# Tying the issue of a half-tile load to a point of the arithmetic, near the end of the store ahead of it

## The chip, the cores and the metric

One core of one Trainium2 chip runs the program. The metric is the device time of an execution in microseconds. The kernel before takes 161.46 us (161.22 to 161.59, three runs).

## The reference

```python
# x: (16, 512, 16, 64) fp32; cos, sin: (512, 32) fp32
x1, x2 = x[..., :32], x[..., 32:]
first  = x1[..., :16] * cos[..., :16] - x1[..., 16:] * sin[..., :16]
second = x1[..., :16] * sin[..., :16] + x1[..., 16:] * cos[..., :16]
out = concatenate([first, second, x2], axis=-1)
```

Half of every row is rotated and the other half is copied. The input is 33.55 MB and so is the output: all of it must be read from HBM (the chip's main memory) into SBUF (the core's working memory) and written back.

## The kernel before

The data is cut into four tiles of 8.39 MB (128 partitions, 16 rows of 1024 numbers each). A ring of three tiles lies in SBUF; VectorE, the engine that does the arithmetic, works in place, in pieces of eight rows (tile 2's second half in five and three). SyncE issues the loads and most of the stores; the DMA engines move the data. Tile 3 takes the place of tile 0 and so has to wait until tile 0 is stored. Tile 2 has a place of its own from the start, but its second half is loaded only behind the first store, so that the DMA engines have work while SyncE waits for that store to land.

```python
def load(t, lo=0, hi=K):
    return nc.sync.dma_start(out=rows(t, lo, hi), in_=xf[t, :, lo * R : hi * R])

def store(t, lo=0, hi=K, queue=nc.sync):
    return queue.dma_start(out=of[t, :, lo * R : hi * R], in_=rows(t, lo, hi))
# ... (tables of cos and sin are loaded and spread)
load(0); load(1); load(2, 0, KC)          # KC = 8, K = 16, KM = 13
# ...
rotate(0, 0, KC)      # four VectorE instructions: mul (L96), mul (L97), sub (L98), add (L101)
rotate(0, KC, K)
store(0)
load(2, KC, K)
load(3)
rotate(1, 0, KC)
rotate(1, KC, K)
behind_loads = store(1)
rotate(2, 0, KC)
near = rotate(2, KC, KM)
rotate(2, KM, K)
store(2, queue=nc.gpsimd)
# behind_loads is made to wait for near ("the store follows the loads at the DMA engines")
rotate(3, 0, KC)
rotate(3, KC, K)
store(3)
```

So the kernel already holds one transfer back: the store of tile 1 waits for a point in tile 2's arithmetic close to the end of the last load.

Of the kernel before, what the change touches and what calls it, by code (L numbers as in the profile page):

```python
# [1 line left out]

# [4 lines left out]


@with_exitstack
def kernel(  # L10
    ctx: ExitStack,
    tc: tile.TileContext,
    x: bass.AP,
    cos: bass.AP,
    sin: bass.AP,
    out: bass.AP,
):
    nc = tc.nc
    fp32 = mybir.dt.float32
    P = 128  # L20
    B, S, H, D = x.shape
    Q = D // 4
    HF = D // 2



    K = 16
    T = B * S // (P * K)
    PB = S // K
    REP = P // PB  # L30
    R = H * D
    NS = 3
    KC = K // 2
    KM = 13

    xf = x.rearrange("b s h d -> (b s h d)").rearrange("(t p f) -> t p f", t=T, p=P)
    of = out.rearrange("b s h d -> (b s h d)").rearrange("(t p f) -> t p f", t=T, p=P)
    cosf = cos.rearrange("(p k) j -> p (k j)", k=K)
    sinf = sin.rearrange("(p k) j -> p (k j)", k=K)

    const_pool = ctx.enter_context(tc.tile_pool(name="const", bufs=1))
    b_pool = ctx.enter_context(tc.tile_pool(name="bp", bufs=1, space=bass.MemoryType.PSUM))


    ring = const_pool.tile([P, NS, K, H, D], fp32)
    stage = const_pool.tile([P, 2, K, HF], fp32)
    spun = const_pool.tile([P, 2 * K, Q], fp32)
    packed = const_pool.tile([PB, 2 * K, Q], fp32)
    table = const_pool.tile([P, 2, K, 2, Q], fp32)

    def rows(t, lo, hi):
        return ring[:, t % NS, lo:hi].rearrange("p k h d -> p (k h d)")
# [8 lines that stand above are left out]
    nc.vector.memset(stage[:, :, :, 0:Q], 0.0)  # L61
    spread = stage.rearrange("(j b) t k i -> j b t (k i)", b=REP)
    nc.gpsimd.dma_start(out=spread[:, 0, 0], in_=cosf)  # L63
    nc.gpsimd.dma_start(out=spread[:, 0, 1], in_=sinf)  # L64
    load(0)
    load(1)
    load(2, 0, KC)




    PQ = PB // REP
    nc.vector.stream_shuffle(  # L73
        out=spun[:],
        in_=stage.rearrange("p t k j -> p (t k) j")[:, :, 0:Q],
        mask=[j % PQ * REP for j in range(PB)],
    )
    for q in reversed(range(REP)):
        n = PQ * (q + 1)
        nc.vector.tensor_copy(out=packed[0:n], in_=spun[q * PB : q * PB + n])  # L80

    for r in range(REP):
        nc.vector.tensor_copy(  # L83
            out=table[r * PB : (r + 1) * PB].rearrange("p t k c j -> p (t k) c j"),
            in_=packed.unsqueeze(2).to_broadcast((PB, 2 * K, 2, Q)),
        )
    C = table[:, 0].rearrange("p k c j -> p k (c j)")
    Sn = table[:, 1].rearrange("p k c j -> p k (c j)")

    def rotate(t, lo, hi):  # L90
        x1 = ring[:, t % NS, lo:hi, :, 0:HF]
        c = C[:, lo:hi].unsqueeze(2).to_broadcast((P, hi - lo, H, HF))
        s = Sn[:, lo:hi].unsqueeze(2).to_broadcast((P, hi - lo, H, HF))
        b_full = b_pool.tile([P, KC, H, HF], fp32, name="b_t")
        b_t = b_full[:, 0 : hi - lo]
        nc.vector.tensor_mul(out=b_t, in0=x1, in1=s)  # L96
        nc.vector.tensor_mul(out=x1, in0=x1, in1=c)  # L97
        nc.vector.tensor_sub(  # L98
            out=x1[:, :, :, 0:Q], in0=x1[:, :, :, 0:Q], in1=b_t[:, :, :, Q:HF]
        )  # L100
        return nc.vector.tensor_add(  # L101
            out=x1[:, :, :, Q:HF], in0=x1[:, :, :, Q:HF], in1=b_t[:, :, :, 0:Q]
        )

    rotate(0, 0, KC)
    rotate(0, KC, K)
    store(0)
    load(2, KC, K)
    load(3)
    rotate(1, 0, KC)  # L110
    rotate(1, KC, K)
    behind_loads = store(1)
    rotate(2, 0, KC)
    near = rotate(2, KC, KM)
    rotate(2, KM, K)
    store(2, queue=nc.gpsimd)

    tc.add_manual_dep(
        behind_loads.ins,
        near.ins.name,  # L120
        mybir.DependencyInfo(mybir.DependencyClass.Sync, mybir.DependencyReason.DATA),
        reason="the store follows the loads at the DMA engines",
    )
    rotate(3, 0, KC)
    rotate(3, KC, K)
    store(3)


# [1 line left out]
_INS = ['x', 'cos', 'sin']  # L130
_OUTS = [((16, 512, 16, 64), 'float32')]


# [23 lines left out]
```

## Time and profile before

| | before |
|---|---|
| median time | 161.46 us |
| span of the profiled run | 159.5 us |
| VectorE busy | 112.9 us, 71% |
| DMA engines busy, both queues | 98.1% |
| bytes read and written | 33.69 and 33.55 MB |

The prediction below shows the lines of this profile. One more view is used throughout, the trace's packet records: each of the 16 engines moves a tile as packets of one partition row, 64 KB for a whole tile (2.418 us each when nothing disturbs) or 32 KB for a half tile (1.213 us). What a packet takes beyond that, averaged over the 16 engines, is time lost on the DMA path (the **excess**). These records are in the packed trace; `prof` sums them up but doesn't print them one by one.

I call the place where a transfer of one direction follows one of the other a **seam**.

### The profile page before, as it was taken

To read this page: it belongs to the slowest core of one execution; us is meant where nothing else is said; L and a number is where in the kernel's file an instruction comes from. 1 tells how busy PE (TensorE), PEld (TensorE's weight loads), DVE (VectorE), ACT (ScalarE), POOL (GpSimd) and SP (SyncE) were. 2 spreads that over 40 slices of the span, in tenths; PEclk is the share of its full clock that TensorE was granted. 3 is DMA by queue.
4 is the path that set the end of the run, shared out by engine and by line. 5 is a ranking of instruction groups with operands and counts; after the bars stand their busy time and mean duration, and the time that the engine had idled before them with its cause. 6 is when DMAs were issued, how large, how long until landed. Compare 5 with 4: busy or idle time off the path is not lost.

```text
span 159.5 us, 115 instructions
## 1 busy us (share of the span) xinstructions
DVE 112.9 (71%) x47; POOL 1.9 (1%) x7
## 2 busy tenths in 40 slices
DVE  1000959999999999999999999999999990000000
POOL 3000000000000000000000000010000000000000
DMA  7969979899699699699996996996996996998966
GB/s 263 542 263 542 444 345 526 362 427 526 271 493 551 263 526 526 263 395 427 493 526 263 526 526 263 526 526 263 526 526 263 526 510 279 526 427 362 526 263 263
DMA packets 1360, 67.24 MB, mean 422 GB/s; under 512 B 176, under 2 KB 176, under 8 KB 208
## 3 DMA queue, kind: packets, MB, share of 16 engines
q1 hardware_dynamic: 1152, 58.72, 85.7%
q0 software_dynamic: 208, 8.52, 12.4%
HBM read 33.69 MB, written 33.55 MB: 422 GB/s over the span
## 4 chain that ended last, share of the span: by engine, by line
DVE 61%; DMA 14%; issue 5%; DVEq 1%
DVE b_t L96 22%; DVE ring L97 22%; DMA ring<-in_x_dram 14%; DVE ring L101 10%; DVE ring L98 7%; DVEq L152 1%; DVEq L96 0%
## 5 line engine op out<-in xcount | busy, mean ns | idle before, releaser
L96 DVE TENSOR_TENSOR b_t<-ring,table 128x4096 f32<-128x4096 f32 (+2 forms) x9 | 35.6, 3959 | 2.1 <-DMA ring<-in_x_dram 1.9
L97 DVE TENSOR_TENSOR ring<-ring,table 128x4096 f32<-128x4096 f32 (+2 forms) x9 | 35.6, 3950 | 0.3
L98 DVE TENSOR_TENSOR ring<-ring,b_t 128x2048 f32<-128x2048 f32 (+2 forms) x9 | 18.4, 2050 | 0.3
L101 DVE TENSOR_TENSOR ring<-ring,b_t 128x2048 f32<-128x2048 f32 (+2 forms) x9 | 18.4, 2043 | 0.0
L73 DVE LOAD_MASK_SELECT spun<-stage x1 | 0.0, 14 | 14.4 <-DMA stage<-in_sin_dram 14.4
L83 DVE COPY table<-packed 32x1024 f32<-32x1024 f32 x4 | 2.7, 684 | 0.1
L58 POOL DMA_DIRECT2D out_dram<-ring x1 | 0.6, 559 | 101.7 <-DVE ring L101 101.7
L80 DVE COPY packed<-spun 32x512 f32<-32x512 f32 (+3 forms) x4 | 1.7, 416 | 0.1
L61 DVE MEMSET stage<- 128x512 f32 x1 | 0.5, 485 | 0.9 <-PEq L141 0.9
L73 DVE STREAM_SHUFFLE spun<-stage 128x512 f32<-128x512 f32 x1 | 0.7, 722 | 0.0
L63 POOL DMA_DIRECT2D stage<-in_cos_dram x1 | 0.6, 642 | 1.3 <-DVE stage L61 1.3
L64 POOL DMA_DIRECT2D stage<-in_sin_dram x1 | 0.5, 532 | 0.0
L141 POOL MEMSET const-bfloat16-1.0<- 128x1 bf16 x1 | 0.1, 101 | 0.0
L141 POOL MEMSET const-float32-0.0<- 128x1 f32 x1 | 0.1, 98 | 0.2 <-issue 0.2
L141 POOL MEMSET const-float32-1.0<- 128x1 f32 x1 | 0.1, 98 | 0.0
L141 POOL MEMSET const-uint8-127<- 128x1 uint8 x1 | 0.1, 98 | 0.0
## 6 DMA issues: line engine op xcount, KB each, us to landing
ring<-in_x_dram SPq DMA_DIRECT2D x2, 4096.0 KB, 40.7
stage<-in_cos_dram POOLq DMA_DIRECT2D x1, 64.0 KB, 8.9
stage<-in_sin_dram POOLq DMA_DIRECT2D x1, 64.0 KB, 13.3
ring<-in_x_dram SPq DMA_DIRECT2D x3, 28.9
out_dram<-ring SPq DMA_DIRECT2D x3, 27.4
out_dram<-ring POOLq DMA_DIRECT2D x1, 39.5
```

Source lines behind the costliest of these rows:

```text
L58: return queue.dma_start(out=of[t, :, lo * R : hi * R], in_=rows(t, lo, hi))
L61: nc.vector.memset(stage[:, :, :, 0:Q], 0.0)
L63: nc.gpsimd.dma_start(out=spread[:, 0, 0], in_=cosf)
L64: nc.gpsimd.dma_start(out=spread[:, 0, 1], in_=sinf)
L73: nc.vector.stream_shuffle(out=spun[:], in_=stage.rearrange("p t k j -> p (t k) j")[:, :, 0:Q], mask=[j % PQ * REP for j in range(PB)],)
L80: nc.vector.tensor_copy(out=packed[0:n], in_=spun[q * PB : q * PB + n])
L83: nc.vector.tensor_copy(out=table[r * PB : (r + 1) * PB].rearrange("p t k c j -> p (t k) c j"), in_=packed.unsqueeze(2).to_broadcast((PB, ...
L96: nc.vector.tensor_mul(out=b_t, in0=x1, in1=s)
L97: nc.vector.tensor_mul(out=x1, in0=x1, in1=c)
L98: nc.vector.tensor_sub(out=x1[:, :, :, 0:Q], in0=x1[:, :, :, 0:Q], in1=b_t[:, :, :, Q:HF])
L101: return nc.vector.tensor_add(out=x1[:, :, :, Q:HF], in0=x1[:, :, :, Q:HF], in1=b_t[:, :, :, 0:Q])
L152: with _tile.TileContext(nc) as tc:
```

## The change

The load of tile 2's second half (the **half load**) is no longer queued right behind the first store, with all of that store's 20 us still ahead. It is issued when the first multiply of tile 1's second half ends, about three microseconds ahead of the end of the store. The same helper replaces the tie of the second store, which keeps its point.

```diff
-        nc.vector.tensor_mul(out=b_t, in0=x1, in1=s)
+        begun = nc.vector.tensor_mul(out=b_t, in0=x1, in1=s)
...
-        return nc.vector.tensor_add(
+        done = nc.vector.tensor_add(
...
+        return begun, done
+    def behind(transfer, point):
+        tc.add_manual_dep(transfer.ins, point.ins.name, ...)
...
     store(0)
-    load(2, KC, K)
+    rest = load(2, KC, K)
     load(3)
     rotate(1, 0, KC)
-    rotate(1, KC, K)
-    behind_loads = store(1)
+    behind(rest, rotate(1, KC, K)[0])
+    last = store(1)
     rotate(2, 0, KC)
-    near = rotate(2, KC, KM)
+    behind(last, rotate(2, KC, KM)[1])
...      (the old tc.add_manual_dep of the second store is removed)
```

More of the change, by code (lines that the diff above doesn't have):

```diff
@@ L100, in rotate @@
         )
-        return nc.vector.tensor_add(
+        done = nc.vector.tensor_add(
             out=x1[:, :, :, Q:HF], in0=x1[:, :, :, Q:HF], in1=b_t[:, :, :, 0:Q]
+        )
+        return begun, done
+    def behind(transfer, point):
+        tc.add_manual_dep(
+            transfer.ins,
+            point.ins.name,
+            mybir.DependencyInfo(
+                mybir.DependencyClass.Sync, mybir.DependencyReason.DATA
+            ),
+            reason="issue the transfer near the end of the one in front of it",
         )
@@ L107 @@
     store(0)
-    load(2, KC, K)
+    rest = load(2, KC, K)
     load(3)
     rotate(1, 0, KC)
-    rotate(1, KC, K)
-    behind_loads = store(1)
+    behind(rest, rotate(1, KC, K)[0])
+    last = store(1)
     rotate(2, 0, KC)
-    near = rotate(2, KC, KM)
+    behind(last, rotate(2, KC, KM)[1])
     rotate(2, KM, K)
     store(2, queue=nc.gpsimd)
-    tc.add_manual_dep(
-        behind_loads.ins,
-        near.ins.name,
-        mybir.DependencyInfo(mybir.DependencyClass.Sync, mybir.DependencyReason.DATA),
-        reason="the store follows the loads at the DMA engines",
-    )
     rotate(3, 0, KC)
```

## The prediction

> **What bounds the kernel now.** One core, 161.46 us (161.22 to 161.59). I read the head of the page first, then the DMA queues, then bandwidth by stretch, and only then the chain.
>
> ```profile
> span 159.5 us, 115 instructions
> DVE 112.9 (71%) x47; POOL 1.9 (1%) x7
> q1 hardware_dynamic: 1152, 58.72, 85.7%
> q0 software_dynamic: 208, 8.52, 12.4%
> HBM read 33.69 MB, written 33.55 MB: 422 GB/s over the span
> ```
>
> VectorE is busy for 71% of the span. The two DMA queues hold the 16 DMA engines for 85.7 + 12.4 = 98.1% of it. The bytes are the problem's own: four tiles of 8.39 MB read once and written once, 67.1 MB. The only open question is whether the rate could be higher. I cut the span at the packets' own starts (a window that cuts packets gives false swings, which is why the 40 slices of the page read 263 and 526 in turn). Columns: length, VectorE and GpSimd busy, a clock of no use here, DMA share, GB/s.
>
> ```profile
> 26.80:38.90 12.10, 12.00 (x5) 0.00 (x0) 1.00 1.00 433
> 53.40:65.50 12.10, 12.00 (x5) 0.00 (x0) 1.00 1.00 433
> 65.50:73.25 7.75, 7.68 (x3) 0.00 (x0) 1.00 0.99 406
> 73.25:80.50 7.25, 7.21 (x3) 0.00 (x0) 1.00 1.00 434
> 107.05:128.80 21.75, 21.58 (x7) 0.00 (x0) 1.00 1.00 434
> 133.70:155.50 21.80, 0.00 (x0) 0.00 (x0) 1.00 1.00 433
> ```
>
> Loads alone (first row), the first store alone (second), two stores from two queues (fifth): all run at 433 to 434 GB/s with the engines full. VectorE is idle in the last row and the rate is the same, so VectorE does not share in the bound. One row is lower: 406 GB/s between 65.50 and 73.25, where the first store ends and tile 2's second half (I call it **the half load**) begins. That is the place the change touches.
>
> ```profile
> 49.87 0.35 SPq L58 DMA_DIRECT2D out_dram<-ring  x1
> 49.88 4.43 DVE L96 TENSOR_TENSOR b_t<-ring,table 128x4096 f32<-128x4096 f32 x1
> 50.26 21.82 SPq L55 DMA_DIRECT2D ring<-in_x_dram  x2
> 63.33 4.43 DVE L96 TENSOR_TENSOR b_t<-ring,table 128x4096 f32<-128x4096 f32 x1
> SPq L55 <- DMA out_dram<-ring: 21.0, 1, 21.0
> ```
>
> The first four lines are the timeline, the last is SyncE's own waits. SyncE issues the first store at 49.87 and the half load at 50.26; the merged "x2" ends with the load of tile 3, which waited 21.0 us for the store to land and was issued at 71.76. The chain of waits on the page is 61% VectorE and only 14% DMA; I discount it, because it follows the last instruction back through VectorE and does not account for the last store's 27 us of data. The last store is issued at 131.19 and lands at 158.58, since the two stores ahead of it are still moving.
>
> **What the Trainium skill says.** "DMA: Bandwidth & Descriptors", section "Where 436 GB/s comes from", gives a ceiling of 435.2 GB/s for a core's 16 DMA engines; the 433 to 434 above agrees, so no reordering can raise the rate of the full stretches. The same page, "Queues, rings and completion order", says descriptors of one queue are consumed in ring order on each engine. The trace agrees: the half load was issued 0.4 us behind the store, yet the store landed 21.9 us after its issue (71.7) and the half load 31.1 us after (81.3), 9.6 us later, its own 4.19 MB at full rate. "Perfetto Trace Analysis", section "DMA Instruction — HWDGE (DVE, Sync)", says the profiled window of a DMA excludes the data movement; the trace agrees, 0.35 us of issue against 21.9 us to landing. No page says what a read queued behind a write on the same queue costs at the seam.
>
> **The change part by part.**
>
> *Removed:* nothing. Same instructions, same bytes, same queues. The tie of the second store to tile 2's 5-row piece is only rewritten through the helper.
>
> *Added:* one wait, of SyncE, on the first multiply of tile 1's second half. That multiply already posts its completion to VectorE's counter in the trace, so VectorE pays nothing. On the path: 0 us.
>
> *Moved:* the half load's issue, from 50.26 to the end of that multiply, 63.33 + 4.43 = 67.76, plus some 0.03 us: 67.79. VectorE runs without a gap from 22.99, so this moment does not move by itself.
>
> *Is the issue in time?* In the trace's packet records the store's last 64 KB packets start between 67.93 and 68.45 and end between 70.74 and 71.25 (landing 71.74). On an idle queue at the start of the kernel, the first load was issued at 0.74 and its first packets began at 1.74 to 2.17: 1.0 to 1.4 us. So the half load can begin at 67.79 + 1.0 to 1.4 = 68.8 to 69.2, which leaves 1.5 us before the earliest engine is free. No bubble.
>
> *What follows it on SyncE:* the tile 3 load still waits for the store's landing at 71.74, 3.5 us after the half load's issue is over (67.79 + 0.43 = 68.22). Its data is not due until the half load is through at 80.5, so there are about 9 us to spare. The half load itself is due when VectorE writes the second half of tile 2 at 90.2, against landing at 81.3: 9 us of slack. Tile 3 lands at 100.7 and is used at 104.3. All stay as they are.
>
> *What can be gained:* only the seam. The 65.50 to 73.25 stretch moved 406 x 7.75 = 3147 KB, which at 433 GB/s would take 7.27 us: 0.48 us lost, read at the first engine. Averaged over the engines, the packet records say less: the sixteen last store packets took 2.42 to 3.32 us in place of 2.418, 0.31 us in the mean, and the first load packets another 0.04: 0.35 us. The seams the other way, load to store at 51 and at 100, show packets at 2.42 us, no loss. So the intent must be that a load queued early takes something from the store in front at its end. If all of it came back: 161.46 - 0.35 = 161.1.
>
> The sum of the parts: 0 on the path, between 0 and -0.35 at the seam.
>
> **The rivals.**
>
> *A, the seam is inherent.* A read following writes costs 0.3 us however long it has been queued: by the time the last packets run (from 68.8) the half load is queued in either version. For: the loss falls on the last packets alone, and the store's earlier packets, with the load queued behind them for 18 us, took exactly 2.418. Against: the last packets that started earliest (67.93 to 68.28) suffered most, and these begin before the delayed load could arrive, so they might be spared. Time 161.4 to 161.5.
>
> *B, the early queueing caused it,* and the delay gives it back: 161.1. For: the point just made. Against: nothing in the trace shows how an engine would see so far ahead.
>
> *C, a cold start takes its place.* The kernel's first packets took 2.89 to 3.45 us, median 3.16, 0.74 more than later ones. If the load is queued too late to be read ahead, a cost of this kind could replace the 0.35: 161.8. Against: 1.5 us of lead, more than the issue needs. If the store, now alone, ended 1 us earlier, the lead would shrink but hold.
>
> *D, a late VectorE delays the load.* A chain of VectorE work now sets when data starts moving. Each us that multiply ends beyond about 70 costs a us of idle DMA. Against: its input landed at 42.2 and it starts at 63.33 behind unbroken work; nothing slower is in sight.
>
> **Range and chances.** I weigh A at 0.55, B at 0.3, C and D together at 0.15. With 161.45, 161.1 and 161.8 that gives 88.80 + 48.33 + 24.27 = 161.40. Three runs of the kernel before spread over 0.37 us, as much as the whole effect, so 8 in 10 lie between 160.9 and 161.8. Faster by 2% would need 3.2 us; the DMA engines' idle time in all the span is about 159.5 x 1.9% = 3.0 us, most of it ahead of the first packet and behind the last, so no version with these bytes can do it. Slower by 2% would need rival D at 3 us. Chances: faster 0.01, same 0.98, slower 0.01.
>
> **What would show it.** Right: SyncE's half load at about 67.8, the tile 3 load at about 71.7, the last store still at 131.2 and landing near 158.5, VectorE's busy time 112.9, and windows over the middle again at 433. The seam tells A from B: about 406 GB/s in the 7.75 us behind 65.5 is A, 420 or more is B, under 395 is C. Wrong: an idle stretch of the DMA engines between 70 and 73, a wait of VectorE for tile 2 or 3 that was not there, or a rate over 435 anywhere, which would break the ceiling I rest on.

## The result, and the profile after

The changed kernel takes 161.76 us (161.46 to 162.09, six runs) against 161.44 us (161.22 to 161.62, six runs). The ratio is 1.0019 with a 95% interval of 1.0005 to 1.0033. (A ratio is the mean time of one kernel's fast runs over that of the other's of the same rounds, so it is not quite the ratio of the medians.) That is the same within 2%, and some 0.3 us slower.

The head of the page of the changed kernel and its DMA queues:

```profile
span 159.9 us, 115 instructions
DVE 112.9 (71%) x47; POOL 1.9 (1%) x7
q1 hardware_dynamic: 1152, 58.72, 85.6%
q0 software_dynamic: 208, 8.52, 12.3%
```

The number of instructions and VectorE's busy time have not moved, and the DMA share is 97.9% after 98.1%: nothing was added to the work. The timeline of the changed kernel, followed by SyncE's own waits (waited for: us in total, times, longest):

```profile
50.06 0.35 SPq L58 DMA_DIRECT2D out_dram<-ring  x1
...
63.51 4.43 DVE L96 TENSOR_TENSOR b_t<-ring,table 128x4096 f32<-128x4096 f32 x1
67.97 3.88 SPq L55 DMA_DIRECT2D ring<-in_x_dram  x2
SPq L55 <- DVE b_t L96: 17.5, 1, 17.5
SPq L55 <- DMA out_dram<-ring: 3.2, 1, 3.2
```

The change did what it meant to. The half load left at 67.97, right at the end of the multiply. SyncE's 21.0 us of waiting for the store's landing turned into 17.5 us of waiting for VectorE and 3.2 us for the landing. The same windows as in the prediction, around the seam and behind it (length, VectorE, GpSimd, clock, DMA share, GB/s):

```profile
65.50:73.25 7.75, 7.68 (x3) 0.00 (x0) 1.00 0.98 389
73.25:80.50 7.25, 7.21 (x3) 0.00 (x0) 1.00 1.00 434
107.05:128.80 21.75, 21.58 (x7) 0.00 (x0) 1.00 1.00 434
133.70:155.50 21.80, 0.00 (x0) 0.00 (x0) 1.00 1.00 433
```

Away from the seam the ceiling of 433 to 434 GB/s is untouched. At the seam the rate reads 389 in place of 406. This figure has to be taken with care: the windows' edges lie between packets in the trace of before, but the engines were 0.8 us apart in this run, and the edges cut packets. The packet records say it better: in this run the store's last packets lost 0.26 us per engine (0.35 before) and the half load's first two lost 0.35 us (0.03 before), 0.62 in all against 0.39. Whether that difference belongs to the change or to the run is what the experiments had to tell.

### The profile page after: what moved, and what is told of

It reads as the page before. It is cut to its first block, busy times and chain, and to the rows that moved or that the text cites. A ratio compares the mean times of both kernels' runs of the same rounds, so it can differ in the third digit from the quotient of the medians.

```text
span 159.9 us, 115 instructions
## 1 busy us (share of the span) xinstructions
DVE 112.9 (71%) x47; POOL 1.9 (1%) x7
## 4 chain that ended last, share of the span: by engine, by line
DVE 61%; DMA 14%; issue 5%; DVEq 1%
DVE b_t L96 22%; DVE ring L97 22%; DMA ring<-in_x_dram 14%; DVE ring L101 10%; DVE ring L98 7%; DVEq L158 1%; DVEq L96 0%
```

## The experiments

Theory 1, **cold start**: a load queued shortly ahead of its turn begins slowly, so it pays at its head what it no longer takes from the store's tail, and more. Rival 1: the tie itself, or something away from the seam, costs the 0.3 us. Rival 2: the change costs nothing and the seam merely varies from run to run. Each call ran on one chip beside its own runs of the kernel before: 161.62 us in the first call (four kernels), 161.77 in the second (four), 161.57 in the third (three), and 161.55 with one more run of it in the last.

### 1. The changed kernel again, twice

No edit; two more chips.

> The changed kernel once more, as the yardstick of this chip and these rounds. If the 0.3 us is real: 161.7 to 161.8 against 161.4 to 161.5, and again first packets of the half load at 1.3 to 2.1 us in place of 1.21. If it was chance of the first measurement: 161.45 and an interval that holds 1.000.

> The changed kernel a third time, on a third chip: 1.0010 to 1.0020 of before if the loss is real, with some 0.3 to 0.4 us of excess per engine in the first two groups of half-load packets.

Measured: a_again 161.82 us, ratio 1.0015 (1.0002 to 1.0027); a_third 161.64 us, ratio 1.0006 (0.9977 to 1.0034). The first narrowly excludes 1.000, as the first measurement did; the second, on a chip with wider scatter (before ran from 161.14 to 162.62), cannot tell. The excess at the half load's head was there both times, 0.33 and 0.28 us per engine. But the store's tail had lost only 0.08 and 0.03 us, so the seam cost 0.41 and 0.31 us in all, in the mean over the engines: about the 0.39 of before. (Section 3 looks at the slowest engine, where it is not quite so.)

### 2. The tie kept, the lead made longer

```diff
-    rotate(1, 0, KC)
-    behind(rest, rotate(1, KC, K)[0])
+    behind(rest, rotate(1, 0, KC)[1])      # early63; early54 takes [0]
+    rotate(1, KC, K)
```

> Half load tied to the end of tile 1's first half (63.3 us on the timeline of before), so about 4.5 us earlier than in the changed kernel, some 6 us ahead of the first free engine. Cold start theory (the load came too late to be read ahead): the loss is gone, 161.4 to 161.5, the same as before. Rival, the tie itself or something else than the lead costs: still 161.7 to 161.8.

> The half load tied to the first multiply of tile 1 (54.3 us), 16 us ahead of the store's end, only 4 us behind the point of before. It has the tie and the long lead. Lead theory: 0.9995 to 1.0007 of before, excess at the store's tail as before and under 0.1 us per engine in the first load packets. Rival, the tie itself costs: 1.0015 to 1.0020.

Measured: early63 161.64 us, ratio 1.0005 (0.9992 to 1.0018), issued at 63.30; early54 161.59 us, ratio 0.9992 (0.9971 to 1.0012), issued at 54.53. The issue of early63 and what it waited for:

```profile
63.30 8.65 SPq L55 DMA_DIRECT2D ring<-in_x_dram  x2
SPq L55 <- DVE ring L101: 13.1, 1, 13.1
```

With the tie and a long lead the time is that of before, so the tie itself costs nothing that these runs can see, as VectorE's unchanged 112.9 us said. The excess is back at the store's tail (0.34 and 0.52 us) and nearly gone from the half load's head (0.06 and 0.10). On the two chips where both were run, the changed kernel's mean was 0.16 us above early63 and 0.23 us above early54: the right sign for theory 1, but only about two standard errors on the first chip and one on the second. The recorded spans, from the first to the last instruction, scatter less: on the first chip the changed kernel has 159.6 once and 159.9 four times, early63 159.4 to 159.7 in six runs and before 159.4 to 159.8 in eleven. On the second chip they overlap (159.4 to 160.4 against 159.4 to 159.6, before up to 160.5).

### 3. The lead made shorter

```diff
+    idle = const_pool.tile([P, 512], fp32)
+    nc.gpsimd.memset(idle[:], 0.0)
+    nc.scalar.copy(out=idle[:], in_=idle[:])      # d692 only
...
-    behind(rest, rotate(1, KC, K)[0])
+    point = rotate(1, KC, K)[0]       # d653: the end of rotate(1, 0, KC)
+    for n in range(2):                # d653: 4
+        pause = nc.scalar.copy(out=idle[:], in_=idle[:])
+        if n == 0:
+            behind(pause, point)
+    behind(rest, pause)
```

ScalarE is idle in this kernel, so a few copies on it serve as a clock that leaves VectorE's stream alone.

> The issue of the half load put between the two points tried, with VectorE's stream untouched: four small copies on the idle ScalarE behind the end of tile 1's first half (63.3), so at about 65.5 to 66, data ready from about 67. If the cost is a matter of lead, the first load packets' excess lies between that of the early run (0.07 us per engine in the two packet groups) and that of the changed kernel (0.34 to 0.37), and the time between: 161.5 to 161.8.

> Two such copies behind the changed kernel's own point (67.8), so the issue falls at about 69 and the first data at 70.0 to 70.4, just as the engines come free (70.3 to 71.0). If a late load only has a cold start: the store's last packets keep 2.418 us (no excess at the tail), the first load packets carry 0.5 to 0.6 us, and the time is 161.6 to 161.9. If the lead must cover more than the issue: above 162.2.

> As d690, but with ScalarE's table loaded at the start, so that the two copies put the issue at about 69.2 and the first data at 70.2 to 70.7, just as the engines come free (70.4 to 71.0): the latest point without idle engines. If the tail is lost only where the load is queued before the store's last packets are under way: tail 0, first load packets 0.5 to 0.6 us per engine, 1.001 to 1.002 of before, as the changed kernel. If both losses add up: 1.004 and more.

Measured: d653 161.77 us, ratio 0.9992 (0.9960 to 1.0025); d690 162.90 us, ratio 1.0066 (1.0033 to 1.0098); d692 162.02 us, ratio 1.0015 (0.9991 to 1.0039). The first two missed their points, and the timeline of d690 shows why: ScalarE loaded a table first, and only once the wait was over.

```profile
67.98 1.28 ACT L128 ACT_TABLE_LOAD   x1 [67.98 <-DVE b_t L98]
69.28 1.27 ACT L128 COPY idle<-idle 128x512 f32<-128x512 f32 x2
70.57 1.20 SPq L57 DMA_DIRECT2D ring<-in_x_dram  x2
```

So d690 issued at 70.57, when the first engines were already free, and d653 at 67.52, 0.4 us ahead of the changed kernel: it became a fourth look at about that point rather than one between. d692, with the table loaded beforehand, hit 69.27:

```profile
67.98 1.27 ACT L129 COPY idle<-idle 128x512 f32<-128x512 f32 x2 [65.33 <-DVE b_t L99]
69.27 2.56 SPq L58 DMA_DIRECT2D ring<-in_x_dram  x2
```

The late72 run ties the half load to the second multiply of the same piece, 4.4 us behind the changed kernel's point:

```diff
-        begun = nc.vector.tensor_mul(out=b_t, in0=x1, in1=s)
-        nc.vector.tensor_mul(out=x1, in0=x1, in1=c)
+        nc.vector.tensor_mul(out=b_t, in0=x1, in1=s)
+        begun = nc.vector.tensor_mul(out=x1, in0=x1, in1=c)
```

> Half load tied to the end of the second multiply of tile 1's second half, 72.2 us. Engines are free at 70.7 to 71.3, data can start at 73.2 to 73.6, so an idle stretch of 2.0 to 2.9 us, and the cold first packets (0.7 us) behind it: 164.0 to 165.0 against 161.45. If data moved late cost nothing, 161.5.

Measured: 166.11 us, ratio 1.0278 (1.0263 to 1.0293), more than any part of the expectation. Windows of this run, the gap first, then tile 3's last packets:

```profile
70.80:73.30 2.50, 2.46 (x2) 0.00 (x0) 1.00 0.00 0
100.50:104.40 3.90, 3.83 (x4) 0.00 (x0) 1.00 1.00 269
```

No packet begins in the 2.5 us of the first row; averaged over the engines the idle time is 2.98 us, and the half load's cold first packets add 0.56. The second row was not expected: tile 3's last packets took 3.89 us in the mean in place of 2.418, 1.47 us lost. The second store is tied to VectorE, which was on time (99.00 us), while the loads were now late; so that store was issued 1.6 us before tile 3's last packets began (100.63), where in before it came 1.4 us behind their beginning (98.86 against 97.43). That this took the time from the loads is what section 5 tests. The parts add up: 2.98 + 0.56 - 0.39 (the seam of before) + 1.47 = 4.6 us, against 4.5 us measured.

The seam of all these runs, from the packet records, in us per engine: excess of the store's last packets, idle time between, excess of the half load's first two packets, and the sum. The column "last" is the loss of the slowest engine: from the latest start of a last store packet to the latest end of the half load's second packets, less the 4.844 us that these packets take undisturbed (2.418 + 2 x 1.213). The last column is the time of the profiled run itself; each row is one execution.

```
run       issued   tail   idle   head   sum    last   its time
before    50.26    0.35   0.01   0.03   0.39   0.39   161.40
early54   54.53    0.52   0.01   0.10   0.63   0.35   161.62
early63   63.30    0.34   0.02   0.06   0.41   0.35   161.59
d653      67.52    0.55   0.01   0.17   0.72   0.91   162.21
a_third   67.75    0.03   0.01   0.28   0.31   0.36   161.31
a_again   67.86    0.08   0.01   0.33   0.41   0.45   161.72
after     67.97    0.26   0.01   0.35   0.62   0.69   162.09
d692      69.27    0.00   0.00   0.76   0.77   0.98   162.33
d690      70.57    0.00   1.08   0.61   1.68   1.56   162.88
late72    72.39    0.00   2.98   0.56   3.53   3.32   166.25
```

Three things are to be seen in the means. The store's tail suffers only where the load is queued before its last packets or just as they start (67.9 to 68.7): from 69.27 on it is exactly undisturbed. The half load's head loses the more the shorter the lead, from 0.03 us in before to 0.76 in d692. And at the changed kernel's own point, the middle four rows, the sum runs from 0.31 to 0.72 us, around 0.52; in the three early rows above it from 0.39 to 0.63, around 0.48. By the means there is no difference worth the name.

But a run ends with its slowest engine, and the column "last" tells another story. Queued early, the seam cost that engine 0.35 to 0.39 us (0.36 also in no_tie2 of section 5, whose half load is queued as in before). The engines that lose most at the tail were ahead of the others: in these four traces the last one to start its last store packet lost 0.01 us or less, and those ahead fell back just behind it. At the changed kernel's point the slowest engine lost 0.36 to 0.91 us. From there on to the end of the last packet all the rows down to d692 took the same 84.53 us, and from the end of the kernel's first packets to the seam all rows took 63.12 to 63.14 us; so within the span nothing away from the seam differs, which rules out that half of rival 1 (early63 and early54 ruled out the tie). The slow profiled runs are those with a large loss in this column; some 0.3 us of further scatter comes from the kernel's first packets, whose latest end lies between 5.27 and 5.58 us. A loss of 0 to 0.5 us that varies from run to run is thus what these few traces show of the changed kernel's point, partly rival 2 and partly theory 1.

### 4. The same point, another queue

```diff
-    rest = load(2, KC, K)
+    rest = load(2, KC, K, queue=nc.scalar)     # load gets a queue argument, as store has
```

act633 is the same with the tie of early63.

> The half load at the same point as in the changed kernel, but on ScalarE's DMA queue, so that from 68.8 on the engines take turns between the store's last packets and the load's. If the seam (0.35 us before, about 0.6 after) comes of a queue having nothing ready but reads that have not arrived, the store's packets fill it: 161.1 to 161.3. If it is inherent in going from writes to reads: 161.4 to 161.8.

> Half load on ScalarE's DMA queue, issued at 63.3, so that its packets take turns with the last three store packets, then with tile 3's load. If mixing hides the seam: no excess at the store's tail or at the first load packets, and 161.1 to 161.3, the best so far. If the half load is again held up by tile 3's packets (one 64 KB packet between every two of its 32 KB): it lands near 88 to 90, VectorE needs it at 90.2, and the time is 161.4 to 162. If the store's landing is late (75) so that the tile 3 load leaves a gap: over 162.

Measured: act678 165.12 us, ratio 1.0218 (1.0205 to 1.0231); act633 161.94 us, ratio 1.0004 (0.9970 to 1.0037). The seam was not hidden. In act678 the half load's packets began only behind the store's last ones, and the seam cost 0.63 us in the mean. Each engine's last store packet was under way by 68.56, less than the 1.0 us behind the issue (67.94) that first data took elsewhere, so this run could not mix the two; act633 could. The 3.5 us came from elsewhere. The timeline of act678, the landing of the half load (KB, us), the piece of VectorE's work that waited for it, and the second store:

```profile
67.94 0.37 ACTq L55 DMA_DIRECT2D ring<-in_x_dram  x1
71.56 0.33 SPq L55 DMA_DIRECT2D ring<-in_x_dram  x1
ring<-in_x_dram ACTq DMA_DIRECT2D x1, 4096.0 KB, 26.0
94.06 2.83 DVE L96 TENSOR_TENSOR b_t<-ring,table 128x2560 f32<-128x2560 f32 x1 [3.74 <-DMA ring<-in_x_dram]
102.70 0.34 SPq L58 DMA_DIRECT2D out_dram<-ring  x1
```

With two queues, each engine took, once tile 3's load had come, one 32 KB packet of the half load and one 64 KB packet of tile 3 in turn. The half load landed 26.0 us after its issue, at 93.97 in place of 81.3; VectorE waited 3.74 us for it, the tied second store went out at 102.70 in place of 98.86, and the DMA engines, through with all loads by 100.8, stood idle until 103.55. In act633 the half load had most of its packets done before tile 3's load came, landed at 89.0, and no one waited: the second case of its expectation. Its mixed packets show a second thing (windows before, at and behind the first mixing):

```profile
53.40:65.60 12.20, 12.10 (x5) 0.00 (x0) 1.00 0.99 430
65.60:69.93 4.33, 4.29 (x2) 0.00 (x0) 1.00 1.00 363
69.93:85.60 15.67, 15.57 (x5) 0.00 (x0) 1.00 1.01 435
```

The first meeting of store and load costs as much as a seam (0.71 us per engine by the records); behind it each engine's one remaining store packet (0.03 us of excess) and the load packets run at the full rate.

### 5. The other seam, and two more

no_tie2 is the kernel before without its own tie; two_seams is the kernel before with the first store and the half load cut in two:

```diff
-    tc.add_manual_dep(behind_loads.ins, near.ins.name, ...)      # no_tie2
```

```diff
-    store(0)                                                     # two_seams
-    load(2, KC, K)
+    store(0, 0, KC)
+    load(2, KC, 12)
+    store(0, KC, K)
+    load(2, 12, K)
```

> The kernel before with its own tie taken away, so the second store is queued at 76.7, far ahead of the end of tile 3's load. The other seam, reads then writes. From the late run, where the store came 4 us early and tile 3's last packets took 3.88 us in place of 2.42: here too some 1.4 to 1.5 us in the last load packets, 162.9 to 163.1. If that loss was something else of the late run: 161.5.

> The kernel before with its first store and the half load each cut in two and queued in turn (store, load, store, load), all early: one more seam from writes to reads and one more from reads to writes. If the seams cost what the other runs showed when queued early (0.4 to 0.6 us from writes to reads, 1.0 to 1.5 us from reads to writes), 1.4 to 2.1 us more than before: 163.0 to 163.7. If the seam is not a matter of the change of direction but of one transfer meeting the end of another at 70 us: within 0.3 us of before.

Measured: no_tie2 163.00 us, ratio 1.0070 (1.0031 to 1.0109); two_seams 162.99 us, ratio 1.0080 (1.0050 to 1.0110). Tile 3's last packets in the kernel before, then in no_tie2, the same 1.05 MB in each row:

```profile
97.40:99.83 2.43, 2.40 (x3) 0.00 (x0) 1.00 1.00 432
```

```profile
97.55:100.85 3.30, 3.23 (x3) 0.00 (x0) 1.00 1.04 318
```

A store queued 20 us ahead, behind loads, took 1.0 us per engine from the last load packets; issued at 98.86, as before has it, it takes none. (From the end of the half load's second packets to the last packet's end no_tie2 took 85.75 us in place of 84.53.) So the tie of before is worth about 1.1 us (0.7%), and the pattern that the change copies does pay at that seam. That is the reason why one might expect it to pay at this one. Windows of two_seams: the first seam, the packets behind it, and the stretch that holds the next two seams:

```profile
48.60:52.15 3.55, 3.52 (x2) 0.00 (x0) 1.00 0.99 295
52.15:61.85 9.70, 9.63 (x4) 0.00 (x0) 1.00 1.00 432
61.85:76.40 14.55, 14.45 (x5) 0.00 (x0) 1.00 1.01 432
```

The sum came out near the lower end of what was expected, but for another reason. The whole loss lies at the first seam, reads to writes, where the first half-store had been queued (at 36.40) 12 us ahead of the load packets that lost: 1.1 us per engine. The seams behind it cost 0.1 us or nothing, even the ones from writes to reads, whose loads had been queued 25 us and more ahead, and which cost 0.39 in the kernel before. Costs of seams therefore do not simply add. Why these were free is not shown: they came behind one that had been paid for, but their packets are also half as long.

## Why the prediction was right

**The bound.** Right, and it decided the case. The DMA engines were full before and after (98.1 and 97.9%), undisturbed packets took the same 2.418 us in every run (16 engines x 65,536 bytes in that time are 434 GB/s), and no version came out clearly faster. The best ratio was 0.9992 with an interval that holds 1.

**The added wait costs nothing on the path.** Right, as far as these runs can tell: the tie with a long lead (early63, early54) gave 1.0005 and 0.9992.

**The issue is in time, no bubble.** Right: it was due at 67.79 and fell at 67.75 to 67.97 in three traces, and the engines' idle time at the seam was 0.01 us each time. That data can begin 1.0 us behind an issue held in the runs that were too late: issued at 70.57 and 72.39, first packets at 71.53 and 73.35.

**The slack behind it.** Right: the half load landed at 81.8, tile 3 at 101.1, the last store was issued at 131.4, and VectorE waited for nothing new. act678 and late72 show what lies beyond that slack.

**What can be gained, 0 to -0.35.** The tail's loss was indeed given back in two of the three traces of the changed kernel (0.03 and 0.08 in place of 0.35), so rival B was right about where it comes from. It was wrong about the sum, because rival C's cold start took its place, at 0.28 to 0.35 us rather than the 0.74 of the kernel's first packets. Rival A, that the seam keeps its size, holds for the mean over the engines: 0.31 to 0.62 in these three traces against 0.39 to 0.63 with an early load. The slowest engine, which sets the time, paid 0.36 to 0.69 against 0.35 to 0.39. The prediction kept the three apart as rivals; they turned out to be parts of one sum. It also misread one size: the store's last packets in the trace of before lost 0.35 us in the mean, not 0.31, and the seam 0.39, not 0.35; the median of these sixteen packets is 0.30 over 2.418. And it summed means, of which the slowest engine need not give anything back.

**Where it was off.** Measured were 161.76, 161.82 and 161.64 against 161.40 predicted. The mixture leaned towards a gain (B at 0.3), and there was none; the figure of C, 161.8 at 0.15 together with D, came nearest. The three ratios taken together, each weighted by the width of its interval, give about 1.0016 (1.0007 to 1.0025), an estimate of ours: a loss of 0.1 to 0.4 us is likely real. d653's 0.9992, issued 0.4 us earlier, neither shows nor excludes it. The first time, 161.76, lies in the range of 160.9 to 161.8 and a_again's 161.82 just outside it, on a chip where before took 161.62. That the number fell inside owes something to luck; that the change would not move the time by 2% does not.

**A poor test.** The prediction meant to tell its rivals apart by the rate between 65.50 and 73.25. That window was cut to fit the packets of one trace. It read 389 in after (C's figure) but 406 in a_again and a_third (A's), the same kernel three times, and 406 also in d692, whose seam cost 0.77 us. For the same reason its last sign of being wrong, a rate over 435 anywhere, did appear: the windows 26.80:38.90 and 53.40:65.50 of after read 439, with edges that cut packets, though undisturbed packets took 2.418 us there too. The excess of the packets, and that of the slowest engine above all, was the measure to name.

**"The seams the other way show no loss."** True of the two in that trace, where both stores had been queued about 1 us ahead of their first packets. With stores queued long before, no_tie2 and two_seams put 1.0 and 1.1 us there.

## What to carry to other kernels

When the DMA engines are full from end to end, as here, holding a transfer back can gain at most what is lost where reads and writes meet, at this seam some 0.4 us of 160; look at whether the loss disappears or turns up at the head of the next transfer before counting it as a gain, and look at the slowest engine, not only at the mean. Each meeting has to be tried by itself: holding a store back behind loads was worth 1.1 us in this kernel, holding a load back behind a store gained nothing and seems to have cost about 0.2 us. A tie to another engine's clock also has a sharp late edge, 0.7% for an issue 2.6 us behind the changed kernel's and 2.8% for 4.4 us, while a long lead cost nothing.

## What the Trainium skill lacked or had wrong

- "DMA: Bandwidth & Descriptors", section "Rules for kernel authors", advises to issue a DMA early and wait late. No page says that a transfer queued early behind one of the other direction slows that one's last packets: 1.0 us per engine for a store behind loads (no_tie2), 0.34 to 0.55 us for a load behind a store, and nothing at all where it was queued during the last packets (d692, d690). It is not always so: the two loads of two_seams, queued 25 us and more ahead with packets half as long, took nothing from the stores in front. Why, these runs do not show.
- The same page, section "Issuing engines are not separate DMA queues", holds that issuing from several engines only saves time on the sequencer. The packets did share the same engines, as it says, but the choice of queue set their order: with the half load issued at the same point from ScalarE's queue the kernel took 165.12 us, 3.5 us more than before, and the load landed after 26.0 us, while from SyncE's queue it landed 13.8 us after its issue (67.97 to 81.80 in the trace of after).
- The same page, section "Queues, rings and completion order", says that the engines take turns between queues by packets. It does not say what that means for large rows: here one turn was a whole partition row, 2.418 us for 64 KB against 1.213 us for 32 KB, so while both had work, the queue with the smaller rows got a third of the bandwidth (act678).
